# Operand splits moved across attention's borders in a hybrid encoder layer, and a score bank swapped

## The chip, the cores and the metric

One core of a Trainium2 chip runs the whole program. The metric is the device time of one execution in microseconds (us). A core has five engines that run side by side, each through its own queue of instructions, in order: TensorE (PE in the profile; its weight loads are PEld), VectorE (DVE), ScalarE (ACT), GpSimd (POOL) and SyncE (SP). In this kernel SP does nothing but issue transfers. An instruction that has to wait holds up everything behind it in its queue.

## The reference

The input x has 2048 rows of 1024 columns, all in float32. Cut to what matters here:

```python
hmix = rms_norm(x, g_norm1) * (1.0 + scale1) + shift1
proj = hmix @ w_in
q_a, k_a, v_a, q_m, k_m, v_m, o_m, gates = jnp.split(proj, IN_SPLITS, axis=-1)
att = rms_norm(banded_attention(q_a, k_a, v_a, sink), g_attn_out)
...
h_fwd = mlstm_chunkwise(qm, km, vm, i_f, f_f)
h_bwd = flip(mlstm_chunkwise(flip(qm), flip(km), flip(vm), flip(i_b), flip(f_b)))
h_m = rms_norm(h_fwd + h_bwd, g_mlstm_out)
h_m = sigmoid(o_m) * h_m
mix = jnp.concatenate([att, h_m], axis=-1) @ w_out
x = x + gate1 * mix
```

A gated feed-forward block and a last norm follow. banded_attention has 8 query heads over 2 key heads and looks 128 positions to either side in blocks of 128; mlstm_chunkwise scans 16 chunks of 128 positions for each of 4 heads, once in each direction.

## The kernel before

A float32 operand of a large matmul is **split**: ScalarE copies it, rounded, into a high part (`hi`), and VectorE or GpSimd subtracts that from it, which gives the low part (`lo`). A product is then three matmuls, hi by hi, hi by lo and lo by hi (`mm3`, L56 to L58). TensorE's order is written out by hand for the whole kernel. The orders of the other four queues are written out by hand in three stretches only (`pre`, `win` and `rest`); between `win.close()` (L1012) and `rest` (L1233), that is during attention, a planner lays them out when the program is built, from the instructions in the order of the code, what each depends on, and its own estimates of time.

**Filler and beats.** Projections of x are generators in the deque `fill`; each `pull()` takes one matmul of the first generator and puts it between the matmuls of the stage at hand. Each pull is also a **beat**: `put_soon(k, f, ...)` asks for f to be issued k beats later, and `beat()` (L116) counts down the list `soon` and issues what is due. The columns of w_in for a projection are loaded and split in this way: `next_cols` (L263) starts `cols_steps` for the columns after the next, whose load into the tile `wraw` (one buffer) comes at beat 6 and whose split into `whi` (ScalarE) and `wlo` (four pieces on POOL) at beats 40, 45, 50 and 55. `proj_cols` (L257) does the same steps at once, and it too loads into `wraw`.

**The mLSTM** (`mlstm`, within `win`) goes backward over the chunks first, each chunk's new state being read out of a bank of PSUM (the memory that TensorE writes) by VectorE (L660); chunk c uses bank `"bcdc"[c % 4]`. Then it goes forward; `scores` takes one matmul of keys by queries for each chunk into bank b or d (L678). Banks b and d have one buffer each; g, a and c have two. After the last head, `first` (four projections) is finished, the list `soon` is emptied by `while soon: beat()` (L1010), and `win` ends. One filler is left in `fill` at that point, `o_first`, and behind it come the last query projection and the gate projections `o_tiles`. A **gate tile** is one 128x512 tile of these: after its 24 matmuls ScalarE takes it out of its bank g by a tanh (L570) into the tile `oth`, and SP writes it out (L571).

**Attention** works through 32 units (16 blocks by 2 key heads). For each unit it loads q, k and v (`aq`, `ak`, `av`, L762 to L766), takes the scores (L782), the exponentials, transposes (L805) split into `apth` and `aptl` (L141, L142), and the value products (L817, L818). Ahead of the first unit come the bias table `abias` (from an iota on POOL) and 36 pulls (L1159).

**The output projection** multiplies by w_out by a scheme with seven products for a pair of row tiles (`out_proj`, L1213). Its seven right-hand operands were prepared earlier in DRAM (`wo_d`); `start_wo(u)` (L1040) loads operand u and `finish_wo(u)` (L1046) splits it: two copies on ScalarE and two subtractions on VectorE, each of 128x1024. The left-hand operands come from `Pair`: `scale` and `sums` make them, `both` splits one of them. Products 1 and 3 use the same bank b1: VectorE reads it out into `xr` (L1225) after product 1, and product 3 goes on adding into it. In code, the places that the diff touches:

```python
    finish_wo(0)                 # L1188, after attention's last unit
...
    pull(10)
    nxt.scale()
    finish_wo(1)                 # L1252
...
    finish_wo(3)                 # L1269
    finish_wo(4)
    finish_wo(5)
    pull(26)
    for _ in range(2):
        nxt.both()
    while fill:
        pull()
    start_wo(6)
```

Of the kernel before, what the change touches and what calls it, by code (L numbers as in the profile page):

```python
# [36 lines left out]
def hybrid_layer_kernel(  # L37
# [14 lines left out]
    def bank(tag, name):  # L52
        return pp.tile([P, 512], F32, tag=tag, name=name, bufs={"g": 2, "a": 2, "b": 1, "c": 2, "d": 1}[tag])
# [56 lines left out]
    soon = []  # L110
# [5 lines left out]
    def beat(k=1):  # L116
        for e in soon:
            e[0] -= k
        due = [e for e in soon if e[0] <= 0]
        soon[:] = [e for e in soon if e[0] > 0]  # L120
        for _, f, args in sorted(due, key=lambda e: e[0]):
            f(*args)

    def pull(n=1):

        while n > 0:
            if not fill:
                n -= 1
                beat()
            elif next(fill[0], None) is None:  # L130
                fill.popleft()
            else:
                n -= 1
                beat()

    def finish_fill(g):
        while any(f is g for f in fill):
            pull()
# [9 lines left out]
    def big(i, name, shape=(P, 2, 512), dt=F32R):  # L148

        return hp.tile(list(shape), dt, tag=f"big{i}", name=name)  # L150
# [431 lines left out]
    def load_v(h, n):  # L582
        va = s2.tile([P, 4, 129], F32, tag="mv", name="mv", bufs=2)
        sp.dma_start(va, vaug_d[n * 512:(n + 1) * 512, h, :].rearrange("(c p) d -> p c d", p=P))
        return va

    def load_qk(h, j, n):
        t = s2.tile([P, 512], F32, tag="mqk", name="mqk", bufs=4)
        sp.dma_start(t, qk_d[j, h, n])
        return t  # L590
# [4 lines left out]
    def mlstm(h, nb, nf, last):  # L595
# [5 lines left out]
        def load_bc(cc):  # L601
            bc = s2.tile([P, 4, P], F32, tag="bc", name="bc", bufs=3)
            sp.dma_start(bc.rearrange("p j t -> p (j t)"), bc_d[h, cc].rearrange("j t -> (j t)").partition_broadcast(P))
            return bc
# [3 lines left out]
        def k_chunk(k_c, va_c, d, cc):  # L608
            kn = kns.get(cc)
            if kn is None:  # L610
                tp = bank("a", "ktp")
                pe.transpose(tp[:, :P], k_c, ident)
                kn = kns[cc] = s2.tile([P, P], F32, tag=f"kn{cc}", name="kn", bufs=1)
                act.activation(kn, tp[:, :P], AF.Copy)
            vw = s2.tile([P, 129], F32, tag="vw", name="vw", bufs=4)
            rr = row(d, cc)
            act.activation(vw, va_c, AF.Copy, scale=wT[:, rr:rr + 1])
            return kn, vw
# [8 lines left out]
        def prep(cc):  # L627
            ng = ngs[cc] = s2.tile([P, 2, P], F32, tag="ng", name="ng", bufs=3)
            pool.tensor_tensor(ng, bcs[cc][:, 0:2, :], maskb, ADD)

        def decays(cc):

            for d in range(2):
                rr = row(d, cc)
                act.activation(ngs[cc][:, d, :], ngs[cc][:, d, :], AF.Exp, bias=rT[:, rr:rr + 1])
# [36 lines left out]
        def scores(cc):  # L672
            n, i = divmod(cc, 4)
            if i == 1 and n + 1 < NB:
                blk[n + 1] = (load_qk(h, 0, n + 1), load_qk(h, 1, n + 1), load_v(h, n + 1))
            qt, kt, va = blk[n]
            q_c, k_c, va_c = qt[:, i * P:(i + 1) * P], kt[:, i * P:(i + 1) * P], va[:, i, :]
            s = bank("db"[cc % 2], "sps")  # L678
            pe.matmul(s[:, :P], k_c, q_c, start=True, stop=True)
            sc = s2.tile([P, 2, P], F32, tag="sc", name="sc")  # L680
            dve.scalar_tensor_tensor(sc, s[:, :P].unsqueeze(1).to_broadcast([P, 2, P]), DS, ngs.pop(cc), MUL, MUL)
            kv = k_chunk(k_c, va_c, 0, cc) if cc < NT - 1 else None
            qs = s2.tile([P, 2, P], F32, tag="qs", name="qs")
            pool.tensor_tensor(qs, q_c.unsqueeze(1).to_broadcast([P, 2, P]), bcs.pop(cc)[:, 2:4, :], MUL)
            if cc + 3 < NT:
                bcs[cc + 3] = load_bc(cc + 3)
            if cc + 2 < NT:
                prep(cc + 2)
            if cc + 1 < NT:
                decays(cc + 1)  # L690
            return (cc, sc, qs, va_c), kv
# [49 lines left out]
        for cc in range(NT + 1):  # L741
            tick()
            if cc == NT - 3 and h + 1 < HM:
                last = load_last(h + 1)
            new = None
            if cc < NT:
                new, kv = scores(cc)
                pull(4)
                if kv:
                    state(cc, kv)  # L750
            pull(nf - 6)
            if todo:
                products(*todo)
            todo = new
# [252 lines left out]
        pull(5)  # L1007
    for g in first:
        finish_fill(g)
    while soon:  # L1010
        beat()
    win.close()  # L1012
    assert len(fill) == 1 and not later
    s2s.close()
# [25 lines left out]
    def start_wo(u):  # L1040
        hl = [[big(4 * u + 2 * z + i, "wo") for i in range(2)] for z in range(2)]
        wo.append(hl)
        for i in range(2):
            sp.dma_start(hl[1][i].bitcast(F32), wo_d[u, 2 * i:2 * i + 2].rearrange("k p t -> p k t"))

    def finish_wo(u):  # L1046
        for hi, lo in zip(*wo[u]):
            act.activation(hi, lo.bitcast(F32), AF.Copy)
            dve.tensor_tensor(lo, lo.bitcast(F32), hi.bitcast(F32), SUB)
# [136 lines left out]
            next(chain0, None)  # L1186
    assert next(chain0, None) is None and len(wo) == 2
    finish_wo(0)  # L1188
    s3s.close()


# [57 lines left out]
        start_wo(u)  # L1249
    pull(10)  # L1250
    nxt.scale()
    finish_wo(1)  # L1252
    nxt.sums(nxt.t.rearrange("p k t -> p (k t)"))
    nxt.both()
    nxt.both()
# [11 lines left out]
    xr.append(load_xr(nxt.tt + 1))  # L1267
    nx3.load_a()
    finish_wo(3)  # L1269
    finish_wo(4)  # L1270
    finish_wo(5)
    pull(26)
    for _ in range(2):
        nxt.both()
    while fill:
        pull()
    start_wo(6)
    for _ in range(2):
        nxt.both()
# [685 lines left out]
```

## Time and profile before

| what | us |
|---|---|
| median of three runs | 2279.1 (2277.12 to 2284.74) |
| the profiled execution | 2279.69 |
| its span, first to last instruction | 2277.8 |
| TensorE busy in it | 2224.1 |
| VectorE / ScalarE / GpSimd busy | 1613.4 / 1059.8 / 1070.8 |
| mean granted TensorE clock, as a share of full speed | 0.995 |

Around the change, by the profile: the mLSTM's first score is at 259.0, attention's first score at 586.5, its last at 783.6, and the output projection begins at 818.8.

A row of the timeline has the start and the length in us, the engine, the source line, the operation, the tiles as written and read (out<-in, with buffer and operand numbers left out, so that mA stands for three operands of the pair and mS for the other four), the shapes and a count; in square brackets how long the engine had been idle before it, and what ended that. SPq rows are SP issuing a transfer: they do not show when it lands. A wait for several things is put down to the one that came last.

### The profile page before, as it was taken

To read this page: it belongs to the slowest core of one execution; us is meant where nothing else is said; L and a number is where in the kernel's file an instruction comes from. 1 tells how busy PE (TensorE), PEld (TensorE's weight loads), DVE (VectorE), ACT (ScalarE), POOL (GpSimd) and SP (SyncE) were. 2 spreads that over 40 slices of the span, in tenths; PEclk is the share of its full clock that TensorE was granted. 3 is DMA by queue.
4 is the path that set the end of the run, shared out by engine and by line. 5 is a ranking of instruction groups with operands and counts; after the bars stand their busy time and mean duration, and the time that the engine had idled before them with its cause. 6 is when DMAs were issued, how large, how long until landed. Compare 5 with 4: busy or idle time off the path is not lost.

```text
span 2277.8 us, 32434 instructions
## 1 busy us (share of the span) xinstructions
PE 2224.1 (98%) x10822; PEld 1857.4 (82%) x10822; DVE 1613.4 (71%) x2931; ACT 1059.8 (47%) x2206; POOL 1070.8 (47%) x927
## 2 busy tenths in 40 slices
PE   7999999999999989999999999999999999999998
PEld 4997888888888878788888888788888888888886
DVE  6787677656688887786666776766667665785694
ACT  4533656544677756354445444433333333233452
POOL 1006535334344344436666665656566664692020
PEclk8999999999999999999999999999999999999999
DMA  8577755685766576764343454433333374542452
GB/s 318 174 242 224 229 169 166 185 240 172 206 187 180 173 248 203 261 234 151 109 147 111 154 180 158 161 98 111 97 112 97 111 253 145 167 153 93 146 214 93
DMA packets 352811, 391.28 MB, mean 172 GB/s; under 512 B 21260, under 2 KB 251004, under 8 KB 352644
## 3 DMA queue, kind: packets, MB, share of 16 engines
q1 hardware_dynamic: 352420, 389.18, 52.2%
q8 instruction: 85, 1.39, 0.2%
q14 instruction: 82, 0.67, 0.1%
q10 hardware_dynamic: 224, 0.04, 0.0%
HBM read 269.95 MB, written 119.19 MB: 171 GB/s over the span
## 4 chain that ended last, share of the span: by engine, by line
PE 52%; DVE 3%; issue 1%; DMA 1%; ACT 0%; POOL 0%; SPq 0%; DVEq 0%; ACTq 0%; POOLq 0%
PE fp L57 12%; PE fp L56 12%; PE fp L58 12%; PE fo L58 5%; PE fo L57 5%; PE fo L56 5%; DVE al L1719 1%; PE ops L56 1%; DMA al<-a_d 1%; DVE ra L1862 1%; PE ops L58 1%; PE ops L57 1%; DVE w L1728 0%; DVE T L1419 0%; DMA A<-in_w_ffn_in_dram 0%
## 5 line engine op out<-in xcount | busy, mean ns | idle before, releaser
L498 PE MATMUL gps<-hT,whi 128*128 128x512 f32 x1088 | 395.3, 418 | 0.3 <-DVE cacc L513 0.3
L58 PE MATMUL fo<-w,al 128*128 128x512 f32 x616 | 240.0, 390 | 0.8 <-DVE al L1719 0.8
L57 PE MATMUL fo<-w,ah 128*128 128x512 f32 x616 | 239.7, 389 | 0.0
L56 PE MATMUL fo<-w,ah 128*128 128x512 f32 x616 | 239.7, 389 | 0.0
L498 PE MATMUL gps<-hT,wlo 128*128 128x512 f32 x544 | 226.1, 416 | 0.0
L498 PEld LDWEIGHTS gps<-hT,whi 128*128 128x128 f32 x1088 | 199.3, 189 | 24.5 <-DVE cacc L513 0.7
L56 PE MATMUL fp<-T,S 128*128 128x512 f32 x528 | 206.7, 391 | 1.1 <-ACT s L1615 1.1
L57 PE MATMUL fp<-T,S 128*128 128x512 f32 x528 | 205.8, 390 | 0.0
L58 PE MATMUL fp<-T,S 128*128 128x512 f32 x528 | 205.4, 389 | 0.0
L1719 DVE TENSOR_TENSOR al<-al,ah 128x1024 fp32r<-128x1024 f32 x77 | 117.1, 1525 | 108.2 <-ACT ah L1718 108.1
L1718 ACT ACTIVATE ah<-al 128x1024 fp32r<-128x1024 f32 x77 | 81.6, 1059 | 180.9 <-DMA al<-a_d 173.6
L1458 DVE TENSOR_TENSOR S<-sf,S 128x512 fp32r<-128x512 f32 x86 | 130.4, 1554 | 35.9 <-ACT S L1457 35.6
L1458 DVE TENSOR_TENSOR A<-graw,A 128x512 fp32r<-128x512 f32 x86 | 129.6, 1524 | 15.5 <-ACT A L1457 15.5
L1623 DVE SCALAR_TENSOR_TENSOR g<-t,g 128x512 f32<-128x512 f32 x44 | 43.7, 993 | 133.0 <-ACT t L1622 133.0
L58 PE MATMUL fp<-B,A 128*128 128x512 f32 x352 | 136.9, 389 | 0.0
L56 PE MATMUL fp<-B,A 128*128 128x512 f32 x352 | 136.9, 389 | 0.0
L57 PE MATMUL fp<-B,A 128*128 128x512 f32 x352 | 136.9, 389 | 0.0
L58 PEld LDWEIGHTS fo<-w,al 128*128 128x128 f32 x616 | 115.6, 188 | 25.7 <-DVE al L1719 1.7
L56 PEld LDWEIGHTS fo<-w,ah 128*128 128x128 f32 x616 | 115.6, 188 | 24.1
L57 PEld LDWEIGHTS fo<-w,ah 128*128 128x128 f32 x616 | 115.6, 188 | 24.0
L1462 POOL TENSOR_TENSOR sf<-A,A22r 128x512 f32<-128x512 f32 x43 | 60.9, 1417 | 150.2 <-DMA A22r<-in_w_ffn_in_dram 117.6
L798 POOL TENSOR_SCALAR ap<-ap,adn 128x384 f32<-128x384 f32 (+1 forms) x128 | 71.1, 575 | 122.6 <-PE atp L805 66.0
(418 smaller groups left out, 6174.6 us busy)
## 6 DMA issues: line engine op xcount, KB each, us to landing
al<-a_d SPq DMA_DIRECT2D x77, 512.0 KB, 3.7
wmod<-in_w_mod_dram SPq DMA_DIRECT2D x48, 512.0 KB, 7.1
graw<-in_w_ffn_in_dram SPq DMA_DIRECT2D x43, 512.0 KB, 3.6
a_d<-ka SPq DMA_DIRECT2D x66, 256.0 KB, 4.7
bc<-bc_d SPq DMA_DIRECT2D x64, 256.0 KB, 3.7
hop_d<-n SPq DMA_DIRECT2D x56, 256.0 KB, 4.6
a_d<-u SPq DMA_DIRECT2D x55, 256.0 KB, 4.6
mqk<-qk_d SPq DMA_DIRECT2D x44, 256.0 KB, 3.8
```

The costliest lines, as they stand in the source:

```text
L56: pe.matmul(o, lh, rh, start=first, stop=False, skip_group_check=skip)
L57: pe.matmul(o, lh, rl, start=False, stop=False, skip_group_check=skip)
L58: pe.matmul(o, ll, rh, start=False, stop=last, skip_group_check=skip)
L498: pe.matmul(ps, w[i == 2][:, k, :], hT[n](i == 1, k), start=(k == 0 and i == 0), stop=(k == KT - 1 and i == 2))
L798: pool.tensor_scalar(self.p[g][:, :self.NK], self.p[g][:, :self.NK], dn[:, g:g + 1], 0.0, MUL, ADD)
L1458: dve.tensor_tensor(t[:, 1, :], f, t[:, 0, :].bitcast(F32), SUB)
L1462: pool.tensor_tensor(f1, a21, a22, ADD)
L1623: dve.scalar_tensor_tensor(g0, t0, 1.0, g0, ADD, MUL)
L1718: act.activation(ah, al.bitcast(F32), AF.Copy)
L1719: dve.tensor_tensor(al, al.bitcast(F32), ah.bitcast(F32), SUB)
L1862: dve.tensor_tensor(ra[i], ra[i], xr, ADD)
```

## The change

Four edits. The score bank's letters are swapped, so that even chunks take b and odd ones d. The loop that empties `soon` at the end of `win` goes, so that the steps left in it are issued by the beats that follow, in attention's 36 pulls. `finish_wo(1)` moves from behind `nxt.scale()` in `rest` to attention's end, behind `finish_wo(0)`. `finish_wo(4)` and `finish_wo(5)` move behind the last gate projection's two tiles: the fourth behind 26 more pulls and two operands' splits, the fifth behind the end of the filler.

```diff
@@ -675,7 +675,7 @@
-            s = bank("db"[cc % 2], "sps")
+            s = bank("bd"[cc % 2], "sps")
@@ -1007,8 +1007,6 @@
     for g in first:
         finish_fill(g)
-    while soon:
-        beat()
     win.close()
@@ -1186,6 +1184,7 @@
     finish_wo(0)
+    finish_wo(1)
     s3s.close()
@@ -1249,7 +1248,6 @@
     pull(10)
     nxt.scale()
-    finish_wo(1)
     nxt.sums(nxt.t.rearrange("p k t -> p (k t)"))
@@ -1267,13 +1265,13 @@
     finish_wo(3)
-    finish_wo(4)
-    finish_wo(5)
     pull(26)
     for _ in range(2):
         nxt.both()
+    finish_wo(4)
     while fill:
         pull()
+    finish_wo(5)
     start_wo(6)
```

## The prediction, made before the changed kernel was run

> **What bounds the kernel now.** I read the page's busy times first, then the table of waits for TensorE, then the queues around each place that the diff touches.
>
> ```profile
> PE 2224.1 (98%) x10822; PEld 1857.4 (82%) x10822; DVE 1613.4 (71%) x2931; ACT 1059.8 (47%) x2206; POOL 1070.8 (47%) x927
> ```
>
> TensorE is busy for 2224.1 of 2277.8 us and the change adds or removes none of its work, so it can win only out of 53.7 us of idleness. The table of waits names the stalls near the edits (line and operation waited for, total, times, longest):
>
> ```profile
> PE ops L56 <- ACT mA L1116: 2.4, 2, 1.4
> PE ops L56 <- ACT oth L570: 2.3, 1, 2.3
> ...
> PE as L782 <- DMA ak<-kst_d: 2.1, 1, 2.1
> ...
> PE sps L679 <- DVE cb L660: 1.1, 1, 1.1
> ```
>
> These four are 7.9 us. What the change can win lies in or just behind them; 0.3% of the time, about what a measurement of this kernel can tell from no change, is 6.8 us.
>
> **1. The score bank, L678.** At head 0's turn from backward to forward:
>
> ```profile
> 255.82 0.35 DVE L660 SCALAR_TENSOR_TENSOR cb<-cb,dec,kvp 128x129 f32<-128x129 f32 x1 [0.68 <-PE kvp L622]
> ...
> 257.96 0.75 DVE L513 SCALAR_TENSOR_TENSOR cacc<-gps,cvw,cacc 128x511 f32<-128x511 f32 x1
> ...
> 258.63 0.80 DVE L660 SCALAR_TENSOR_TENSOR cb<-cb,dec,kvp 128x129 f32<-128x129 f32 x2
> ...
> 259.02 0.49 PE L679 MATMUL sps<-mqk 128*128 128x128 f32 x2 [1.06 <-DVE cb L660]
> ```
>
> Score 0 takes bank d, which chunk 2's state left only at 258.98, since VectorE was in a convolution. With the letters swapped it takes b, last used by chunk 4, read out by 256.17. The wait of 1.06 goes; score 1 takes d a whole step later, when it is long free. The next matmuls need ScalarE alone (it was idle there). The other three heads show no such wait, and the last score of a head now leaves d where it left b, which the next head touches later still. I take 1.06, with ends 0 and 1.06.
>
> **2. Attention's start: the weight split left to the beats, L1010.** Now the loop empties the list of due steps at once, in the hand-ordered stretch:
>
> ```profile
> 575.73 1.05 ACT L251 ACTIVATE whi<-wraw 128x1024 fp32r<-128x1024 f32 x1
> ...
> 575.86 0.37 SPq L122 DMA_DIRECT2D mxm_d<-og  x1
> ...
> 576.85 2.82 POOL L254 TENSOR_TENSOR wlo<-wraw,whi 128x256 fp32r<-128x256 f32 x4 [3.44 <-ACT whi L251]
> ...
> 579.70 0.37 SPq L247 DMA_DIRECT2D wraw<-in_w_in_dram  x1
> ...
> 580.17 0.53 SPq L1020 DMA_DIRECT2D skb<-in_sink_dram  x1
> ...
> 581.24 0.50 SPq L764 DMA_DIRECT2D ak<-kst_d  x1
> ...
> 584.01 0.39 PE L498 MATMUL gps<-hT,whi 128*128 128x512 f32 x1
> ...
> 584.37 0.62 DVE L1029 TENSOR_SCALAR abias<-d 128x384 bf16<-128x384 f32 x2
> ...
> 586.53 0.36 PE L782 MATMUL as<-ak,aq 128*128 128x256 f32 x1 [2.13 <-DMA ak<-kst_d]
> ```
>
> SP's queue stands still from 576.23 to 579.70: at its head is the reload of wraw, which may start only when POOL's four pieces have read it (579.67). Behind it wait the sink row and attention's first keys; ak, issued at 581.24, is there about 5.3 us later, and TensorE has nothing from 584.40 to 586.53. With the split among attention's own instructions, the loads stand ahead of it in the code: ak can go at about 577.4 (1.07 behind skb, as now) and land at 582.7, before 584.40. All 2.13 go. The bias table ends at 584.99 even where POOL keeps today's order, in time for the first scores. The pieces themselves (1.05 on ScalarE, 2.82 on POOL) then lie beside TensorE's 36 filler matmuls; their user, the next projection, comes some 60 matmuls after 584. But those queues are ordered by the planner, not by the code: wraw's reload stands ahead of skb although the code names it much later. So it may again come first. Ends: a gain of 2.13, and a loss of 2.1 if the pieces now follow their beats (the last is due some 22 filler matmuls of 0.23 after 576, and takes 0.7: about 581.8 instead of 579.67) with the reload still ahead of ak.
>
> **3. w_out's second split, L1252, goes to attention's end.** Two copies on ScalarE and two subtractions on VectorE leave the stretch behind attention:
>
> ```profile
> 800.74 1.99 ACT L1048 ACTIVATE wo<-wo 128x1024 fp32r<-128x1024 f32 x2
> ...
> 801.81 3.04 DVE L1049 TENSOR_TENSOR wo<-wo 128x1024 fp32r<-128x1024 f32 x2 [1.58 <-ACT wo L1048]
> ...
> 804.75 0.50 PE L1127 MATMUL aps<-ones_r,msq 128*128 128x1 f32 x4
> ...
> 806.47 1.79 DVE L1120 TENSOR_TENSOR mA<-mm,mA 128x512 fp32r<-128x512 f32 x1
> ...
> 808.18 0.15 DVE L99 TENSOR_SCALAR arv<-aps 128x2 f32<-128x2 f32 x1
> ...
> 809.37 1.29 POOL L1109 TENSOR_TENSOR mm<-mm,ms 128x512 f32<-128x512 f32 x1
> ...
> 809.47 1.21 DVE L104 TENSOR_TENSOR ara<-ary 128x2 f32<-128x2 f32 x1
> ...
> 811.10 0.16 DVE L104 TENSOR_TENSOR ara<-ary 128x2 f32<-128x2 f32 x1
> ```
>
> The square root at 808.18 has its input from 805.25 and waits for VectorE alone. Without 3.04 ahead of it, it starts at about 805.35, 2.8 earlier. It then lies more under POOL's sums: the same two-column operation takes 1.21 us while POOL works and 0.16 us after. One such block more than now costs 0.7 to 1, so VectorE reaches the next weight splits some 2 us earlier (810.6, not 812.68).
>
> [...]
>
> In attention the two subtractions land in a crowded place:
>
> ```profile
> 767.00:785.00 18.00, 17.34 (x96) 14.41 (x96) 16.94 (x45) 14.27 (x38) 6.66 (x12) 1.00 0.58 165
> ...
> 780.43 1.22 DVE L1049 TENSOR_TENSOR wo<-wo 128x1024 fp32r<-128x1024 f32 x1
> 782.37 0.50 PE L818 MATMUL ao<-aptl,av 128*128 128x512 f32 x1 [0.66 <-DVE aptl L142]
> 790.10 0.68 DVE L822 TENSOR_TENSOR at<-ao,at 64x512 f32<-64x512 f32 x1 [1.41 <-ACT at L821]
> 793.99 0.68 DVE L822 TENSOR_TENSOR at<-ao,at 64x512 f32<-64x512 f32 x1 [1.63 <-ACT at L821]
> ```
>
> (The first row's columns: stretch, length, then busy time of PE, PEld, DVE, ACT, POOL.) The first split's second half, at 780.43, held up the value matmul by 0.66. The two new ones (1.22 each) fit the holes of 1.41 and 1.63 near the end; I take a loss of 0.4, with ends 0 and 2.44 (both wholly on the path).
>
> **4. Splits 4 and 5 behind the gate tile, L1270.** Split 3 stays; so do the transfers, since they are issued ahead of all this.
>
> ```profile
> 810.68 0.39 PE L498 MATMUL gps<-hT,wlo 128*128 128x512 f32 x1
> ...
> 812.68 9.17 DVE L1049 TENSOR_TENSOR wo<-wo 128x1024 fp32r<-128x1024 f32 x8
> ...
> 813.38 1.06 ACT L1048 ACTIVATE wo<-wo 128x1024 fp32r<-128x1024 f32 x1 [2.56 <-DMA wo<-wo_d]
> ...
> 817.25 1.06 ACT L1048 ACTIVATE wo<-wo 128x1024 fp32r<-128x1024 f32 x1 [0.22 <-DMA wo<-wo_d]
> ...
> 818.22 0.58 ACT L570 ACTIVATE oth<-gps 128x512 f32<-128x512 f32 x1
> ...
> 818.85 0.51 PE L56 MATMUL ops<-wo,mA 128*128 128x512 f32 x1 [2.34 <-ACT oth L570]
> ...
> 824.17 1.65 DVE L1094 SCALAR_TENSOR_TENSOR ma<-ma,cols,arb 128x256 f32<-128x256 f32 x4
> ...
> 825.73 0.68 DVE L1225 TENSOR_TENSOR xr<-xr,ops 128x512 f32<-128x512 f32 x1
> ...
> 826.57 0.47 PE L56 MATMUL ops<-wo,mS 128*128 128x512 f32 x1 [1.39 <-ACT mA L1116]
> ```
>
> ScalarE now does four copies, each behind its transfer, before it empties the gate tile's bank at 818.22; the projection's first matmul needs that bank. The tile before the last ends at 811.07; with the order turned, its bank is read out at about 811.7, in ScalarE's pause of 2.56, and the projection starts when the last tile ends, 818.85 - 2.34 = 816.51. But that is not yet the gain. The third product adds into the first one's bank and so waits until VectorE has read it at 825.73 to 826.41; the name mA in the last row is only what ended nearest. VectorE comes there after eight splits (9.17), four small parts and the scaling (1.65), and the change only reorders these. So the saved 2.34 becomes a longer wait at the third product, and the gain of parts 3 and 4 together is what VectorE wins. From 810.6: splits 2 and 3 (eight in 9.17, so 1.15 each) to 815.2, two parts (four between 821.85 and 824.17, so 0.6 each) to 816.4, split 4 to 818.7, split 5 to 821.0 (its copies follow the last gate tile, 816.51 + 0.58 + 2 x 1.06 = 819.2, and are in time), two parts to 822.2, and the scaling, so that the read-out starts 1.56 later, as now, at 823.7. That is 2.0 earlier; POOL's squares, which a matmul early in the third product needs, move less and may give some back. I take 1.6. Ends: 0, if the root stays as late as now, and 2.5, where split 5's copy at 819.2 is the limit (one subtraction, two parts and 1.56 from there: 823.1).
>
> **The sum**, against the profiled execution's own 2279.69 us (span 2277.8): 1.06 + 2.13 + 1.6 - 0.4 = 4.4, so 2275.3. That execution lies 0.6 above the median of the runs shown (2279.1, from 2277.12 to 2284.74), so I forecast 2275.
>
> **Rivals.**
>
> *The reload still comes first.* The planner hoists copy and pieces to where they are and SP waits as now. For: the split is ready at 575.7, its engines are free, and the reload was already put ahead of skb. Against: the loads are named first. Then 1.06 + 1.6 - 0.4 = 2.3: 2276.8.
>
> *VectorE's lead is lost.* The root is blocked to the end of POOL's sums and both moved subtractions cost in full: 1.06 + 2.13 + 0 - 2.44 = 0.75: 2278.4. Against: the holes in VectorE's rows at 790 and 794.
>
> *All the waits fall.* If VectorE came to its read-out early enough for the third product too, the 1.39 there goes beside the 2.34: 1.06 + 2.13 + 3.73 = 6.9, and the other wait of the pair on mA (2.4 - 1.39) makes 7.9: 2271.2. Against: split 5's copies.
>
> *Slower: attention is planned anew.* Its four queues are laid out by the planner, and the diff changes what enters at its first and last unit. If the new layout puts one VectorE step ahead of the low part in every one of the 32 units, each may lose as at 782.37. It decides from 4.4 / 32 = 0.14 us a unit; at 0.4 (between that and the 0.66 seen) it costs 12.8: 2287.5. For: VectorE has little slack (16.94 of 18). Against: the stall at 782.37 stands beside a split that was moved in, and the diff brings only one more such split and its like at the start.
>
> **How the numbers follow.** Forecast 0.45, reload first 0.25, lead lost 0.08, all fall 0.10, planned anew 0.12. The forecast's own range is 2272.5 to 2277.5. With all but the far ends of the last two: 2270.5 to 2283. Faster by over 0.3% (below 2272.3) needs most of "all fall" and the forecast's edge: 0.14; slower (above 2285.9) most of the last: 0.09; within: 0.77.
>
> **What would show it.** Right: no wait at head 0's turn; SP issuing ak near 577.4 and no wait for ak; no wait behind L570 before the projection; a *longer* wait (2 to 2.5) at the third product; the root at about 805.4. Wrong: wraw's reload still ahead of ak, the root still at 808, or new waits for aptl all through attention.

## The result and the profile after

The changed kernel takes 2273.38 us (median of 16, 2270.97 to 2275.83), the kernel before 2279.41 (median of 16) beside it: ratio 0.997, 95% interval 0.9963 to 0.9977. Two more comparisons, on two other occasions, gave 0.9974 (0.9964 to 0.9984) and 0.9972 (0.9961 to 0.9982). So 6 to 7 us are gone. The forecast, 2275 from a sum of 4.4, had the sign and about two thirds of the size.

The busy times on the page of the changed kernel:

```profile
PE 2222.6 (98%) x10822; PEld 1856.6 (82%) x10822; DVE 1618.5 (71%) x2931; ACT 1059.6 (47%) x2206; POOL 1065.6 (47%) x927
```

The work is the same. The span is 6.2 us shorter (2271.6 against 2277.8): TensorE is idle for 4.7 less and busy for 1.5 less, though its 10822 matmuls are the same. The timeline at head 0's turn and at attention's start (PE, ACT, POOL and SP rows put in order of time):

```profile
257.38 0.38 PE L679 MATMUL sps<-mqk 128*128 128x128 f32 x2
...
566.11 1.06 ACT L251 ACTIVATE whi<-wraw 128x1024 fp32r<-128x1024 f32 x1 [0.21 <-DMA wraw<-in_w_in_dram]
567.25 2.83 POOL L254 TENSOR_TENSOR wlo<-wraw,whi 128x256 fp32r<-128x256 f32 x4 [5.67 <-ACT whi L251]
570.10 0.38 SPq L247 DMA_DIRECT2D wraw<-in_w_in_dram  x1
...
576.46 0.45 SPq L1018 DMA_DIRECT2D skb<-in_sink_dram  x1
577.45 0.51 SPq L764 DMA_DIRECT2D ak<-kst_d  x1
...
582.76 0.28 PE L782 MATMUL as<-ak,aq 128*128 128x256 f32 x1
...
588.40 0.45 PE L782 MATMUL as<-ak,aq 128*128 128x384 f32 x1 [0.47 <-DVE nmx L786]
```

The first score no longer waits for the state, and attention's first score no longer waits for its keys: ak goes out at 577.45, where it went at 581.24. But look at what stands ahead of it: the split that was to be left to attention's beats now runs *earlier*, at 566 instead of 576, inside the mLSTM, and wraw's reload follows it at 570.10. And one score, at 588.40, has a wait of 0.47 for VectorE.

The same view of the stretch behind attention:

```profile
802.15 0.16 DVE L99 TENSOR_SCALAR arv<-aps 128x2 f32<-128x2 f32 x1 [2.21 <-PE aps L1125]
...
807.14 4.62 DVE L1047 TENSOR_TENSOR wo<-wo 128x1024 fp32r<-128x1024 f32 x4
...
809.01 0.82 SPq L1061 DMA_DIRECT2D ma<-mxa_d  x1
...
813.22 0.39 PE L56 MATMUL ops<-wo,mA 128*128 128x512 f32 x1
...
819.65 1.15 ACT L1075 ACTIVATE msq<-ma 128x512 f32<-128x512 f32 x2 [1.99 <-DMA ma<-mxa_d]
...
820.59 0.68 DVE L1224 TENSOR_TENSOR xr<-xr,ops 128x512 f32<-128x512 f32 x1
821.42 0.47 PE L56 MATMUL ops<-wo,mS 128*128 128x512 f32 x1 [2.00 <-ACT mA L1114]
...
823.73 0.38 PE L1125 MATMUL aps<-ones_r,msq 128*128 128x1 f32 x2 [1.27 <-POOL msq L1077]
...
825.18 0.63 PE L56 MATMUL ops<-wo,mS 128*128 128x512 f32 x1
825.61 0.63 PE L57 MATMUL ops<-wo,mS 128*128 128x512 f32 x1
```

The projection starts without a wait (813.22), the third product waits 2.00 for the first one's read-out by VectorE, a matmul behind it 1.27 for POOL's squares, and then the matmuls come 0.43 apart instead of 0.23. The table by stretch shows TensorE's clock there (columns as in the prediction's such row; behind the five busy times stand the granted clock, the DMA share and GB/s):

```profile
823.70:827.70 4.00, 3.97 (x11) 3.15 (x12) 2.72 (x14) 1.06 (x1) 1.22 (x1) 0.57 0.44 157
```

TensorE's granted clock stands at one half from 824.2 to 827.65.

To read several traces against each other, the start of the n-th matmul in one is set against the n-th of before's profile. The lead so found, in us, negative where ahead, at the matmuls that stand at these times before:

| kernel | 256 | 270 | 560 | 586 | 600 | 797 | 826 | 860 | end |
|---|---|---|---|---|---|---|---|---|---|
| before, second trace | 0.0 | 0.0 | 0.0 | -0.5 | 0.0 | 0.0 | 0.2 | 0.1 | -1.0 |
| after | -0.4 | -1.7 | -1.6 | -3.8 | -3.3 | -3.2 | -5.2 | -3.2 | -6.0 |
| after, second trace | 1.4 | 0.1 | 0.0 | -2.2 | -1.9 | -1.8 | -3.8 | -1.5 | -3.6 |
| after, third trace | 2.2 | 0.9 | 1.1 | -1.0 | -0.6 | -0.5 | -2.3 | -2.2 | -4.5 |

The first column is spread of the kernel's own start, ahead of any edit. What the edits do is the difference between neighbouring columns: about -1.3 at the bank, -2.1 at attention's first score with some 0.4 given back by 600, nothing through attention, -2.0 up to the third product, and in two of three traces all of that lost again by 860.

### The profile page after: what moved, and what is told of

The parts are those of the page before. It is cut to its first block, busy times and chain, and to the rows that moved or that the text cites. A ratio compares the mean times of both kernels' runs of the same rounds, so it can differ in the third digit from the quotient of the medians.

```text
span 2271.6 us, 32440 instructions
## 1 busy us (share of the span) xinstructions
PE 2222.6 (98%) x10822; PEld 1856.6 (82%) x10822; DVE 1618.5 (71%) x2931; ACT 1059.6 (47%) x2206; POOL 1065.6 (47%) x927
## 3 DMA queue, kind: packets, MB, share of 16 engines
q8 instruction: 85, 1.39, 0.3%
## 4 chain that ended last, share of the span: by engine, by line
PE 55%; DMA 1%; DVE 1%; issue 1%; POOL 1%; ACT 0%; SPq 0%; POOLq 0%; ACTq 0%
PE fp L56 12%; PE fp L57 12%; PE fp L58 12%; PE fo L57 6%; PE fo L58 6%; PE fo L56 6%; PE ops L56 1%; PE ops L57 1%; PE ops L58 1%; DMA al<-a_d 0%; PE trn L183 0%; DMA T<-hop_d 0%; DMA a_d<-c 0%; DVE T L1417 0%; DMA w2n<-in_w_ffn_out_dram 0%
```

## The experiments

The theory behind the experiments: bank and attention's start win what was predicted; of the two edits behind attention only the second split wins, and the fourth and fifth move TensorE's idle time to a place where it costs more. Changes are shown against the kernel before, unless said otherwise.

**Two halves.** Bank and attention's start:

```diff
-            s = bank("db"[cc % 2], "sps")
+            s = bank("bd"[cc % 2], "sps")
...
-    while soon:
-        beat()
```

> The kernel before with the first two edits alone (the score bank and the split left to the beats). Theory A, the gain sits at head 0's turn and at attention's start: about 1.1 + 2.1 - 0.5 = 2.7 us faster than before (0.12%), with no TensorE wait at the first score and none for ak, and the stretch behind attention as before (a wait of 2.3 behind L570, 1.4 at the third product). Theory B, the rest of the 6 us measured comes from w_out's splits: the same 2.7 here, and some 3 us from the other two edits. Theory C, the four edits work only together: under 1 us here.

and the three moved splits:

```diff
     finish_wo(0)
+    finish_wo(1)
     s3s.close()
...
     nxt.scale()
-    finish_wo(1)
...
-    finish_wo(4)
-    finish_wo(5)
     pull(26)
     for _ in range(2):
         nxt.both()
+    finish_wo(4)
     while fill:
         pull()
+    finish_wo(5)
```

> The kernel before with the last two edits alone (w_out's splits 1, 4 and 5 moved). Theory A: within 1 us of the kernel before, since what the output projection gains at its start (some 2 us at the third product) it gives back when TensorE waits for POOL's squares (1.3) and for a spell of half clock; TensorE's lead over the kernel before, matmul by matmul, is about nothing once the first pair of the projection is done. Theory B: about 3 us faster, the lead kept to the end.

The first half took 2275.48, ratio 0.9979 (0.997 to 0.9988), the second 2278.09, ratio 0.9991 (0.9982 to 0.9999). Both win, and their two means, -4.4 and -2.5 against before beside them, add up to the whole (-6.5 for the changed kernel there), though the second's interval all but reaches 1. By the lead, the first half won 1.35 at the bank, 2.14 at 586, and held 2.9 to the end, less than the means say. The second half in its trace:

```profile
824.55 0.47 PE L56 MATMUL ops<-wo,mS 128*128 128x512 f32 x1 [1.73 <-ACT mA L1116]
825.78 0.38 PE L1127 MATMUL aps<-ones_r,msq 128*128 128x1 f32 x2 [0.19 <-POOL msq L1079]
```

The squares' wait is 0.19 here, no half-clock stretch follows, and 1.8 us are won between 797 and 860.

**Both kernels once more**, for a second trace of each:

> The kernel before, unchanged: ratio 1.000. For the stages that no edit touches, what a second execution of the same program shows: where the spells of half clock fall, and how long the start, the feed-forward block and the last stage take. If the spell near 1445 us (3.4 us long, 1.7 us of matmul time) is there again, it belongs to this kernel; if it falls elsewhere or nowhere, it belongs to the execution.

> The changed kernel, unchanged: 6 us (0.26%) faster than before again. If the spell of half clock at 824 us belongs to the execution, it falls elsewhere or is missing here, and the output projection then keeps the lead of its third product but for the 1.3 us wait for POOL's squares; if it belongs to the kernel (two waits of 2.0 and 1.3 close to each other), it is there again.

They took 2280.0, ratio 1.0004 (0.9995 to 1.0012), and 2273.3, ratio 0.9974. The changed kernel's half-clock stretch is there again, from 824.3, and twice as long: 6.83 us. The stretch near 1445 is there again in before, at 1444.7, and the changed kernel has one there in its second trace (1442.1) that its first had not. The second trace of before has a half-clock stretch as well, at the projection's start:

```profile
820.00:823.50 3.50, 3.50 (x13) 2.88 (x11) 3.50 (x5) 2.36 (x5) 1.58 (x1) 0.51 0.53 156
```

Ahead of it stands the wait for the gate tile:

```profile
818.81 0.50 PE L56 MATMUL ops<-wo,mA 128*128 128x512 f32 x1 [2.32 <-ACT oth L570]
```

There it costs nothing: the slowed matmuls end at the third product, which has to wait for its bank anyway (lead 0.2 at 826). In the changed kernel the stretch lies *behind* that wait, and is paid for.

**The second split alone** (of the diff above, only `finish_wo(1)`):

> The kernel before with the third edit alone (w_out's second split at attention's end). Theory A, VectorE's queue behind attention is what limits the third product: the root starts near 805.4 instead of 808.2 and VectorE's read-out of the first product comes about 2 us earlier; the wait behind L570 at the projection's start stays at 2.3, the wait at the third product (1.4) goes to about nothing, so 1.4 us are won. Rival, the gate tile on ScalarE is the limit: both waits as before, nothing won; attention's end may lose 0.6.

2280.41, ratio 0.9994 (0.9983 to 1.0005). Its trace around the projection's first and third product:

```profile
818.49 0.50 PE L56 MATMUL ops<-wo,mA 128*128 128x512 f32 x1 [2.53 <-ACT oth L570]
...
824.64 0.39 PE L56 MATMUL ops<-wo,mS 128*128 128x512 f32 x1
```

The wait for the gate tile's bank stays, the third product's 1.39 is gone, and the lead grows by 1.6 from 797 to 860. The time can't tell 1.6 from nothing.

**The fourth and fifth alone:**

> The kernel before with the fourth edit alone (splits 4 and 5 behind the gate tile). Theory A: the wait behind L570 (2.3) goes and the wait at the third product grows from 1.4 to about 3.5, because VectorE's work is only reordered: 0 to 0.3 us won when the first pair is done. Rival: the gate tile is the limit, 2 us won and kept.

2282.48, ratio 1.0006 (0.9997 to 1.0016). Its third product:

```profile
827.27 0.77 PE L56 MATMUL ops<-wo,mS 128*128 128x512 f32 x1 [4.08 <-ACT mA L1116]
```

The 2.34 at the gate tile and the 1.39 at the third product have become one wait of 4.08, behind which the clock halves: 1.2 us lost from 797 to 860. Alone, this edit only moves the wait. (This trace also has a half-clock stretch at 586.3, behind the wait of 2.11 for ak, which the edit does not touch; it cost 0.9 by 600.) By the times, the two parts alone, 0.9994 and 1.0006, add up to nothing, where both together had 0.9991; each interval is some 4 to 5 us wide, so neither figure can be leant on.

**The split done early by hand.** Since the planner had put attention's split ahead of where the code names it, this kernel empties the list by hand, three rounds sooner, and keeps all else of before:

```diff
-    for _ in range(6):
+    for i_ in range(6):
         tick()
         pull(5)
+        while i_ == 2 and soon:
+            beat()
```

> The kernel before with the list of due steps emptied three rounds earlier (after the third of the six rounds of five pulls that end the mLSTM), still within the hand-ordered stretch and by hand; nothing else changed. Theory, SP's queue is held by the reload of wraw behind POOL's pieces: the last piece ends some 4 us earlier (about 576), ak is issued near 578 and TensorE's wait for ak falls from 2.1 to 0.2 or less, so about 2 us are won at attention's first score, as with the split given to the planner. Rival, the planner has to have the split for the gain (its other work for attention's start moves with it): the wait for ak stays near 2.

2278.56, ratio 0.9997 (0.9985 to 1.0008), while the reload, the keys and the scores stand so:

```profile
577.23 0.38 SPq L247 DMA_DIRECT2D wraw<-in_w_in_dram  x1
...
580.35 0.63 SPq L764 DMA_DIRECT2D ak<-kst_d  x1
...
585.25 0.28 PE L782 MATMUL as<-ak,aq 128*128 128x256 f32 x1
...
591.17 0.16 DVE L795 TENSOR_TENSOR adn<-adn,ars 128x4 f32<-128x4 f32 x1 [3.39 <-ACT adn L794]
...
591.93 0.44 PE L782 MATMUL as<-ak,aq 128*128 128x384 f32 x1 [1.29 <-DVE nmx L786]
```

The wait for the keys is gone (2.3 won at 586), which shows its cause: the reload's place in SP's queue is harmless if the split it waits for is done early. The keys went out at 580.35, later than the 578 expected, and were still in time. The time itself can't tell 2 us from nothing. By 600, 1.5 of the 2.3 were lost again to VectorE's row maxima: VectorE stood 3.39 behind a small ScalarE step, and the scores behind VectorE. So in this trace the next limit at attention's start lay 1.5 behind the keys; in the kernels with the planner's layout it took less.

**The normalisation's load ahead of the residual's,** laid on the changed kernel, to take away the squares' 1.27:

```diff
-    xr.append(load_xr(nxt.tt + 1))
     nx3.load_a()
+    xr.append(load_xr(nxt.tt + 1))
```

> The changed kernel with two transfers swapped: the attention rows of the pair after next (ma, from which POOL's squares are made) are loaded ahead of the residual rows xr instead of behind them. Theory, in the changed kernel the wait of 1.3 for POOL's squares inside the third product comes from that load's landing, and together with the 2.0 just before it brings the spell of half clock at 824: the load lands about 1.2 us earlier, the wait falls under 0.4, the spell goes, and the first pair of the projection ends 2 to 3 us earlier than in the changed kernel (2270.5 to 2271.5 us). Rival, the landing is set by the amount of data in flight: the wait stays over 1 and the time is that of the changed kernel.

2275.11, ratio 0.9975 (0.9966 to 0.9984). ScalarE's squares came without a wait, and yet:

```profile
818.02 1.14 ACT L1075 ACTIVATE msq<-ma 128x512 f32<-128x512 f32 x2
...
822.50 0.67 PE L56 MATMUL ops<-wo,mS 128*128 128x512 f32 x1 [2.27 <-ACT mA L1114]
...
824.54 0.77 PE L56 MATMUL ops<-wo,mS 128*128 128x512 f32 x1
```

The half clock came all the same, behind the single wait of 2.27, and for 6.83 us. So the squares' wait is not needed for it, and the 2270.5 to 2271.5 expected did not come. That the new order took the squares' wait away is not shown: it is missing in a trace with the old order too (the third, below).

**The first three edits without the fourth and fifth moved** (the changed kernel, with these two back in their old place):

```diff
     finish_wo(3)
+    finish_wo(4)
+    finish_wo(5)
     pull(26)
     for _ in range(2):
         nxt.both()
-    finish_wo(4)
     while fill:
         pull()
-    finish_wo(5)
```

> The bank, attention's start and w_out's second split moved, the fourth and fifth left where they were. Theory A (the fourth and fifth only move TensorE's idle time from the gate tile to the third product, and there the matmul clock drops to one half for 3.4 us behind it, which is paid): the wait behind the last gate tile stays at 2.3 to 2.5, the third product waits less than 0.4, no half-clock stretch between 815 and 830 costs time, and the kernel takes 2273 to 2275, no more than 1 us above the changed kernel or even below it. Theory B (the fourth and fifth add a gain of their own on top of the second): at least 1.2 us slower than the changed kernel, 2275 to 2276.

2276.11, ratio 0.9977 (0.9968 to 0.9986):

```profile
815.93 0.50 PE L56 MATMUL ops<-wo,mA 128*128 128x512 f32 x1 [2.27 <-ACT oth L570]
...
822.08 0.39 PE L56 MATMUL ops<-wo,mS 128*128 128x512 f32 x1
```

In this trace the lead grew by 1.9 from 797 to 860, more than in any trace of the changed kernel, as theory A has it. The medians, 2276.11 against 2274.82 for the changed kernel beside it, lean to theory B, but the intervals of the two ratios overlap over most of their length. So: the fourth and fifth splits make a difference of less than some 2 us to the others, and its sign isn't settled.

**The changed kernel a third time:**

> The changed kernel once more, for a third trace of it. If the half-clock stretch behind the third product's wait is the rule, it stands there again (between 820 and 828) and the stretch from 797 to 860 wins less than 0.5 us against before; if it falls by chance, it can be missing, and that stretch wins 1.5 to 2.5. Time 2273 to 2274 either way.

2274.82, ratio 0.9972, a little above the time expected. The same stretches as above:

```profile
820.03 1.16 ACT L1075 ACTIVATE msq<-ma 128x512 f32<-128x512 f32 x2 [0.35 <-DMA ma<-mxa_d]
...
824.29 0.47 PE L56 MATMUL ops<-wo,mS 128*128 128x512 f32 x1 [2.20 <-ACT mA L1114]
...
825.07 0.50 PE L1125 MATMUL aps<-ones_r,msq 128*128 128x1 f32 x4
```

```profile
823.70:827.70 4.00, 3.41 (x17) 2.93 (x18) 3.76 (x11) 2.94 (x4) 2.31 (x3) 1.00 0.69 231
```

The load came in time, the squares cost nothing, the clock stayed whole, and 1.7 us were won from 797 to 860. The loss seen in the first two traces belongs to the execution, not to the kernel.

**VectorE's order turned around,** on the changed kernel: the next normalisation's load first as above, the first pair's scaling put off from the second output to the fifth, the squares' sums three steps later.

```diff
-        prev, rows, dl = rows, None, int(bool(put_off))
+        prev, rows, dl = rows, None, int(bool(put_off)) if p else 3
...
-            if nxt and i == 1:
+            if nxt and i == (1 if p else 4):
                 nxt.scale()
```

> The changed kernel with the second normalisation's load ahead of the next residual's, the scaling of the first pair put off from the second to the fifth output of the pair's loop, and the squares' column sums three steps later. Theory A (VectorE's order at the third product decides: its read-out of the first product comes first, the scaling after it): the third product's wait falls from 2.0 to under 0.6, the wait for POOL's squares from 1.27 to under 0.4, no half-clock stretch at 824, and 2 to 3 us less than the changed kernel: 2270 to 2272. Theory B (VectorE's total work in the stretch decides, the order only moves the wait to a later product or to the normalised tiles): within 0.7 us of the changed kernel.

2276.94, ratio 0.9981 (0.9972 to 0.999), so not better than the changed kernel. Its trace, VectorE and TensorE:

```profile
822.38 0.47 PE L56 MATMUL ops<-wo,mS 128*128 128x512 f32 x1 [0.55 <-DVE xr L1224]
...
828.93 1.27 DVE L102 TENSOR_SCALAR ar1h<-ar1v 128x2 f32<-128x2 f32 x1
...
830.29 1.27 DVE L105 TENSOR_TENSOR ar1a<-ar1a,ar1h 128x2 f32<-128x2 f32 x1
...
833.97 0.68 DVE L1224 TENSOR_TENSOR xr<-xr,ops 128x512 f32<-128x512 f32 x1
834.71 0.80 PE L56 MATMUL ops<-wo,mS 128*128 128x512 f32 x1 [3.38 <-DVE xr L1224]
```

```profile
834.00:838.00 4.00, 3.29 (x8) 2.62 (x9) 4.00 (x6) 1.16 (x2) 1.27 (x1) 0.50 0.00 0
```

The third product's wait fell from 2.00 to 0.55 as meant. The two slow rows at 828.93 and 830.29 take 1.27 each, where the small steps around them take 0.15 to 0.17; the first of them is a step with one input. POOL is busy for 3.86 us, with three instructions, between 826 and 840; whether they lie beside these two rows is not shown. Twelve us after the third product the square root, put off with the sums, stands ahead of the next read-out and TensorE waits 3.38; the clock halves there. Theory A falls. The trace has theory B's mechanism: VectorE is busy for 14.95 of the 16 us from 818 to 834, and the new order moved the wait to a later product. Theory B's bound, within 0.7 us of the changed kernel, is not shown: the medians are 2.1 apart, with intervals that overlap.

**The same on the first three edits:**

> The same three edits of order on the kernel that leaves the fourth and fifth splits ahead of the gate tile. Theory A: the third product waits for nothing in the kernel they are laid on, so they bring less than 0.7 us to it. Theory B (VectorE's total decides): the same, and this one and the changed kernel with the three edits end within 0.7 us of each other; under theory A the changed kernel with them is 1.2 to 2.4 us ahead of this one, since the wait behind the gate tile is left only here.

2278.92, ratio 0.9984 (0.9974 to 0.9994), with the waits at both places:

```profile
819.14 0.80 PE L56 MATMUL ops<-wo,mA 128*128 128x512 f32 x1 [3.53 <-ACT oth L570]
...
838.55 0.50 PE L56 MATMUL ops<-wo,mS 128*128 128x512 f32 x1 [1.88 <-DVE xr L1224]
```

The wait at the gate tile is 1.3 longer than in the kernel it is laid on, and the median 2.8 above that kernel's, where both theories expected less than 0.7 us of difference; why is not shown. The two kernels with the three edits are 2.0 apart by their medians and 0.7 by their ratios, so this pair does not decide between the theories. No version here beats the changed kernel.

## Why the prediction was right

*The bank.* Predicted 1.06. The wait is gone in all eight traces with the edit, and the lead grows by 1.3 in each. Right in mechanism; 0.3 more than the wait's own length, of which 0.1 is the score itself (0.49 behind the wait, 0.38 without).

*Attention's start.* Predicted 2.13, by the loads standing ahead of the split in the code. The size held: 2.1 to 2.2 at the first score, ak issued at 577.45 against the 577.4 worked out. What bound TensorE, SP held by the reload, was right as well. The step that failed is the reason why SP would come free, and that the time came out all the same is luck. The planner did not follow the code: it pulled the split back into the mLSTM, and the reload still stands ahead of the keys, as the rival "the reload still comes first" had it. That rival took the reload's place for its cost; but the reload waits for POOL's pieces, and those were done at 570. The doubt "those queues are ordered by the planner" was the right one, and its consequence was not thought through. What the prediction left out is who is next: VectorE's row maxima, 0 to 0.5 in the traces of the changed kernel and 1.29 in the split by hand. About 1.7 to 1.9 of the 2.13 last in the changed kernel.

*The second split.* Predicted root at 805.35, weight splits from 810.6. With the lead of 3.16 at that place added, the trace has 802.15 + 3.16 = 805.31 and 807.14 + 3.16 = 810.30. Two steps of the root lie under POOL's sums (802.94 and 804.21, 1.3 each) and end with them:

```profile
803.11 1.15 DVE L105 TENSOR_TENSOR ara<-ara,arh 128x2 f32<-128x2 f32 x1
804.30 1.23 DVE L106 SCALAR_TENSOR_TENSOR ary<-ara,ary 128x2 f32<-128x2 f32 x1
```

The root takes 4.99 us, 0.5 more than before's 4.50 (808.18 to 812.68), not 0.7 to 1: before had a second slow step as well, ahead of the 1.21 that the prediction shows. It takes 0.54 here, and the prediction did not count it:

```profile
808.36 1.08 DVE L101 TENSOR_SCALAR ary<-arv 128x2 int32<-128x2 int32 x1
```

So the weight splits begin 0.3 earlier than worked out. The same two steps take 1.15 and 1.23 where a sum of POOL's runs, and behind the last sum the root's two-input steps take 0.16 or 0.17 each. Predicted loss in attention 0.4; the lead changes by 0.1 from 600 to 797 in all three traces, though the two subtractions did not lie in the holes named. The last of attention's four stands here, beside POOL, whose four steps make TensorE wait for 0.40:

```profile
784.28 1.25 DVE L1047 TENSOR_TENSOR wo<-wo 128x1024 fp32r<-128x1024 f32 x1
...
783.98 2.80 POOL L798 TENSOR_SCALAR ap<-ap,adn 128x256 f32<-128x256 f32 x4 [3.75 <-DVE adn L796]
...
785.93 1.24 PE L805 MATMUL atp<-ident,ap 128*128 128x128 f32 x3 [0.40 <-POOL ap L798]
```

*The fourth and fifth.* Predicted: the 2.34 goes and comes back as 2 to 2.5 at the third product, VectorE's read-out at 823.7. Measured: 2.00, 2.02 and 2.20 in the three traces, read-out at 820.59 + 3.16 = 823.75. The end of VectorE's chain, added up step by step, was good to 0.1 us, but with two errors of 0.3 that cancel: it began 0.3 early, and lost that again on the way, 0.20 of it in a wait for split 5's copy, which the sum had in time. "May give some back", said of POOL's squares, was the mis-sized term: it was put at 0.4 (2.0 to 1.6). The wait was 1.27 in the first trace, 1.25 in the second and 0 in the third. In the first the load of the next normalised operand, issued at 809.01, was awaited until 819.65, 10.6 us; in the second it took 11.0, in the third 8.6. Its issue had not moved ahead with the matmuls; why it landed sooner in the third is not shown. Where the wait fell, a half-clock stretch followed, which the prediction did not have at all. Wait and stretch took 3.0 in the first trace and 4.2 in the second, of which 1.0 and 1.9 came back by 860 at places where before waits too. Parts 3 and 4 together won 1.7 in the third trace and 0 and -0.3 from 797 to 860 in the others.

*The sum.* From the traces: 1.3 + 1.8 - 0.1 + 1.7 = 4.7 where the clock stays whole, 3 where it doesn't, against the predicted 4.4. The closeness is partly luck, since the last term is 1.7, 0 or -0.3. The profiled executions agree: 2273.35, 2275.75 and 2274.82 after, 2279.69 and 2278.74 before, 4.6 between their means, or 5.3 if the spread of the start (the table's first column) is left out. The ratios of the timed runs say 5.9 to 6.8.

What the sum lacks lies in part behind 860, where no edit reaches and the prediction put nothing. From 860 to the end the changed kernel's three traces win 2.8, 2.1 and 2.3, and before's own second trace 1.1. The largest piece is the half-clock stretch at 1445: both traces of before have it, the first and third of the changed kernel don't, and that is 1.6 each. It also shows that "only out of 53.7 us of idleness" was too narrow a bound, since at half clock TensorE is slow while busy. Whether the edits make such stretches rarer is not shown. The mean granted clock listed for each timed run is 0.9947 over 94 runs of before and 0.9951 over 31 of the changed kernel; 0.0004 of 2275 is an estimated 0.9 us of full-speed time, and the difference is only about twice the uncertainty of the two means. The rest, 0.6 to 1.5 us, is not located: single executions of one kernel differ by more (before from 2275.12 to 2285.34), so five profiles can't find it.

*The rivals.* "All the waits fall" came nearest of the rivals in time (2271.2) and was wrong: the third product's wait grew. "Attention planned anew" was right that the planner would lay attention's start out anew, wrong in that each of the 32 units would pay: the lead doesn't move from 600 to 797.

## What to carry to other kernels

Where a planner orders the queues, a piece of work freed from a hand-written place can move earlier as well as later; ask where its inputs are ready, not where the code names it. A load that stood ahead of another in a queue cost only as long as that load itself had to wait: the keys behind the reload cost 2.13 us where it went out at 579.70, and nothing where it went out at 570.10 or 577.23. Where an engine was full over a stretch, adding up its steps in order gave the next wait closely (to 0.1 us at the third product), and a new order on it chose which consumer waits (0.55 at the third product, then 3.38 at a later one). When work is brought forward, ask whether its transfers come with it. And a half-clock stretch seen in one trace is not yet a cost of the kernel: see whether the same wait brings it in a second one (2.27 did in one trace and not in another).

## What the runs showed of the hardware

The half clock around a short wait was not expected. At this projection the granted clock then stands at 0.50, and matmuls come 0.43 apart instead of 0.23, for 3.41 us (first trace of the changed kernel, from 824.2) or twice that (the second, from 824.3). It came with each of the single waits of 3.38 (VectorE's order turned around), 3.53 (the same on the first three edits) and 4.08 (fourth and fifth alone). It came with a wait of 2.32 (second trace of before) but not with 2.34 (the first), with 2.27 where the load was put first but not with 2.27 in the first three edits, and not with 2.20 (third trace) or 2.53 (second split alone). It came both times behind a pair, 2.0 and then 1.3 with only a few matmuls between (first and second trace of the changed kernel).

So the length of a wait does not say by itself whether a stretch follows. Where the stretches fall can be read from the first trace of each of the two kernels. In each, all half-clock stretches begin a whole number of steps of 3.413 us apart (before: 25.29, 52.60, 1445.23 and 2271.26, which are 8, 408 and 242 steps; after: 22.11, 32.35, 824.24 and 2268.08, which are 3, 232 and 423). With each trace cut along these steps, two stretches begin between 200 and 2260 us, one in each trace: behind a step in which TensorE was idle for 2.71 us (before, from 1441.82) and behind one with 1.86 (after, from 820.83). The most idle of the other steps there, 1.67 (before, from 817.18) and 1.71 (after, from 1438.64), had none behind them. Ahead of 200 us one with 1.14 had (before, from 49.18), so two traces give no bound. One place shows that the same wait can end both ways: near 1442 TensorE waits for VectorE for 2.84 us in before and for 2.85 in the changed kernel. Before comes first, with most of the wait in one step, and then the changed kernel, where the border at 1438.64 cuts it (the rows of numbers are such steps):

```profile
1444.53 0.50 PE L57 MATMUL fp<-T,A 128*128 128x512 f32 x1 [2.84 <-DVE T L1419]
1441.82:1445.23 3.41, 0.70 (x3) 0.61 (x4) 3.41 (x3) 0.00 (x0) 0.97 (x1) 1.00 0.00 0
1445.23:1448.64 3.41, 3.41 (x10) 2.63 (x9) 3.41 (x5) 0.00 (x0) 1.60 (x1) 0.50 0.00 0
...
1440.35 0.50 PE L57 MATMUL fp<-T,A 128*128 128x512 f32 x1 [2.85 <-DVE T L1417]
1438.64:1442.05 3.41, 1.70 (x7) 1.43 (x8) 3.41 (x5) 0.00 (x0) 0.00 (x0) 1.00 0.00 0
```

In the first, TensorE is busy for 0.70 us of the step and the granted clock is 0.50 in the next; in the second it is busy for 1.70, and the clock is 1.00 in the next (1442.05 to 1445.46). What decides between them is not shown.

What a stretch costs depends on what comes behind it: 1.6 us at 1445, nothing ahead of a wait for another engine (second trace of before, at 820). At 824, behind the last such wait, it and the squares' wait together left the first and second trace of the changed kernel 1.7 and 2.0 behind the third.
